# Two parts of x in one matmul of 512 columns: the up projection of a decoder layer, column tiles 6 to 21

## The chip, the cores and the metric

The kernel runs on one core of a Trainium2 chip. Its time is device time in microseconds (us) of one execution; the kernel before was run three times and once more under the hardware profiler. The engines are TensorE (PE; PEld is its weight load), VectorE (DVE), ScalarE (ACT), GpSimd (POOL) and SyncE (SP, which issues the DMAs here). Each works through its own list of instructions in order and waits on semaphores for the others.

## The reference, cut to what matters

One decoder layer on 256 rows of 1024 values in float32: a combined input projection, attention, convolution and pooling mixers, an output projection, a LayerNorm, then the gated MLP, which the change touches:

```python
x = layer_norm(DEEPNORM_ALPHA * x + mix, ln1_g, ln1_b)
up = causal_dwconv(x @ w_up, ffn_conv_w) + ffn_conv_b     # three taps along the sequence
u, g = jnp.split(up, 2, axis=-1)
ff = (u * jax.nn.silu(g)) @ w_down
return layer_norm(DEEPNORM_ALPHA * x + ff, ln2_g, ln2_b)
```

`w_up` is 1024 x 5632 (2816 columns for u, 2816 for g), `w_down` 2816 x 1024.

## The kernel before, in words

**Split products.** A float32 product is made of three matmuls in the format fp32r. Each operand a is split into a part `hi` (a copy on ScalarE that rounds, L122) and `lo` = a - hi (a subtraction on VectorE, L123); `mm3` (L149) then sums hi·hi, hi·lo and lo·hi in PSUM. Weights are split as they arrive, in units of 128 x 1024: `wsplit` (L129) issues one hi on ScalarE and one lo on VectorE. x after the first LayerNorm is split once into `xh` and `xl`.

**The MLP.** The 2816 columns of u and of g are cut into 22 column tiles of 128, j = 0 to 21. For tile j, `up_mm(j, 0)` (u) and `up_mm(j, 1)` (g) each run 8 blocks of the contraction with three matmuls of 256 columns (the sequence); the weights are the stationary operand. Both results share one PSUM bank of 512 columns. `taps(j, s)` makes the three-tap convolution: ScalarE writes y = w2·src + bias out of PSUM (L479), VectorE adds the two shifted taps (L480, L481), reading PSUM. `gate_silu` is sg on ScalarE (L485), `gate_out` is f = y0·sg on VectorE (L489), then the split of f into mh (ScalarE, L122) and ml (VectorE, L123). `down_block(k)` multiplies column tile k by its weights: matmuls of 512 columns whose stationary operand is mh or ml, summed over all tiles in four banks that stay occupied for the whole stage. Tile 0 of the up projection is computed apart (`up_first`).

**The order.** It is written out by hand. A list of blocks holds for each block its matmuls, and two lists `a` and `b` of steps for the other engines. The loop at L649 issues a block's matmuls, then the `a` steps of the block before, then weight splits as long as `ready` allows (in this stage one unit per block, six blocks ahead of its use), then the `b` steps of the block before. From tile 5 on a tile is three blocks: up u, up g, down block j - 5 (`LAG`). Down blocks 15 to 21 (`KEEP`) compute only the first half of the rows in their turn; their second half comes at the very end. The PSUM pool has eight banks, and a bank is given out again when the last reader of its old content is done.

Of the kernel before, what the change touches and what calls it, by code (L numbers as in the profile page):

```python
# [10 lines left out]
F32 = mybir.dt.float32  # L11
BF16 = mybir.dt.bfloat16
F32R = mybir.dt.float32r
AF = mybir.ActivationFunctionType
# [3 lines left out]
P = 128  # L18
D = 1024
S = 256  # L20
NT = S // P
KD = D // P
# [3 lines left out]
NJ = FF // P  # L26
# [9 lines left out]
LAG = 5  # L36
KEEP = 7
FIRST = 2
WARM = 23


PIECES = (((0, 512), (512, 512)), ((0, 512), (512, 256), (768, 256)))
# [14 lines left out]
def trunk(ctx, tc, a_qk, a_v, a_cp, a_out, a_up, a_down, x, par, tab, lnp, out):  # L57
    nc = tc.nc
    cp = ctx.enter_context(tc.tile_pool(name="cp", bufs=1))
    wp = ctx.enter_context(tc.tile_pool(name="wp", bufs=WB))  # L60
    rp = ctx.enter_context(tc.tile_pool(name="rp", bufs=RB))
    wk = ctx.enter_context(tc.tile_pool(name="wk", bufs=2))
# [3 lines left out]
    def bank():  # L66
        return ps.tile([P, 512], F32, name="bank")

    def tmp(name):
        return wk.tile([P, S], F32, name=name, tag="t", bufs=12)  # L70

# [8 lines left out]
    for n, i in units:  # L82
        at = {"qk": a_qk, "v": a_v, "cp": a_cp, "out": a_out, "u": a_up, "g": a_up, "d": a_down}[n]
        c = i if n in ("qk", "u", "g") else i // 2
        h = 0 if n in ("qk", "u") else 1 if n == "g" else i % 2
# [35 lines left out]
    def split(raw, hi, lo):  # L121
        nc.scalar.activation(hi, raw, AF.Copy)  # L122
        nc.vector.tensor_sub(lo, raw, hi.bitcast(F32))  # L123
# [25 lines left out]
    def mm3(o, lh, ll, rh, rl, start, stop, skip=False):  # L149
        for i, (l, r) in enumerate(((lh, rh), (lh, rl), (ll, rh))):  # L150
            nc.tensor.matmul(o, l, r, start=start and i == 0, stop=stop and i == 2,  # L151
                             skip_group_check=skip)

    xh = cp.tile([P, KD, S], F32R, name="xh")
    xl = cp.tile([P, KD, S], F32R, name="xl")

    zero = cp.tile([P, P], BF16, name="zero")
    nc.vector.memset(zero, 0.0)
    warm = bank()
    for i in range(WARM):  # L160
        nc.tensor.matmul(warm[:, :P], zero, zero, start=True, stop=True)
# [41 lines left out]
    mh = cp.tile([P, KD, S], F32R, name="mh")  # L203
    ml = cp.tile([P, KD, S], F32R, name="ml")
# [89 lines left out]
    def pool_sums(t, p_ps):  # L294
        p_ps = p_ps[:, :S]

        p, a, b, d = tmp("pin"), tmp("pa"), tmp("pb"), tmp("pd")
        nc.scalar.activation(p, p_ps, AF.Copy)

        def step(dst, src, w, rows):  # L300
            nc.gpsimd.tensor_add(dst[rows, w:], src[rows, w:], src[rows, :S - w])
            nc.gpsimd.tensor_copy(dst[rows, :w], src[rows, :w])

        al, up = slice(0, P), slice(DH, P)
        step(a, p, 1, al)
        if t == 0:
            step(b, a, 2, up)
        else:
            step(b, a, 2, al)
            step(a, b, 4, al)  # L310
            step(b, a, 8, up)
        iw = prm[:, C_IW + t:C_IW + t + 1]
        ed = prm[:, C_ED + 16 * t:C_ED + 16 * t + 16]
        for rows, src in ((slice(0, DH), a), (up, b)):
            nc.gpsimd.tensor_mul(d[rows, :16], src[rows, :16], ed[rows])
            nc.gpsimd.tensor_scalar(d[rows, 16:], src[rows, 16:], iw[rows], None, op0=ALU.mult)
        nc.gpsimd.tensor_sub(d, d, p)
        return d

    def pool_mm(t, d):  # L320
        y_ps = bank()
        nc.tensor.matmul(y_ps[:, :S], prm[:, C_WP + t * P:C_WP + (t + 1) * P], d,  # L322
                         start=True, stop=True)
        y = tmp("py")
        nc.scalar.activation(y, y_ps[:, :S], AF.Copy, scale=prm[:, C_PS + t:C_PS + t + 1])
        to_mix(6 + t, y)

    def conv_z(t, cc_ps, cx_ps):
        cc_ps, cx_ps = cc_ps[:, :S], cx_ps[:, :S]
        cx, z, y = tmp("cx"), tmp("cz"), tmp("cy")  # L330
        nc.scalar.activation(cx, cx_ps, AF.Copy)
        nc.vector.tensor_mul(z, cc_ps, cx)
        w = [prm[:, C_CW + 3 * t + i:C_CW + 3 * t + i + 1] for i in range(3)]
        nc.vector.tensor_scalar(y, z, w[2], None, op0=ALU.mult)
        nc.vector.scalar_tensor_tensor(y[:, 1:], z[:, :S - 1], w[1], y[:, 1:], op0=ALU.mult, op1=ALU.add)
        nc.vector.scalar_tensor_tensor(y[:, 2:], z[:, :S - 2], w[0], y[:, 2:], op0=ALU.mult, op1=ALU.add)
        return y
# [36 lines left out]
    def sum_rows(accs, rows, last, t, p, lh, ll, h, l, i):  # L374

        ts = slice(t * P, (t + 1) * P)
        if len(accs[t]) == 0:
            accs[t].extend((bank(), bank()))
        if t == 1 and p == 2 and len(accs[t]) == 2:
            accs[t].append(bank())  # L380
        whole = p is None or t == 0
        for b in range(2) if p is None else (p,):
            c, n = (b * 512, 512) if whole else PIECES[t][p]
            o = accs[t][b] if whole else accs[t][p][:, :n]
            mm3(o, lh[:, ts], ll[:, ts], h[:, c:c + n], l[:, c:c + n],
                i == 0 or (t == 1 and p == 2 and i == last), i == rows - 1, skip=True)
# [13 lines left out]
    def w_out(t, i, p):  # L400
        h, l = W["out", i]
        kt = order[i]
        sum_rows(acc, KD, FIRST, t, p, mh[:, kt], ml[:, kt], h, l, i)

# [5 lines left out]
    def w_out_last(t, p):  # L410
        for i in range(FIRST, KD):
            w_out(t, i, p)
# [39 lines left out]
    gt = {}  # L452

    def up_mm(j, s):
        h, l = W.pop(("ug"[s], j))
        if s == 0:
            u_ps[j] = bank()
        for k in range(KD):
            ws = slice(k * P, (k + 1) * P)
            mm3(u_ps[j][:, s * S:(s + 1) * S], h[:, ws], l[:, ws], xh[:, k], xl[:, k], k == 0, k == KD - 1)  # L460
# [10 lines left out]

    u_ps, ys = {}, {}

    def taps(j, s):
        c = s * NJ + j
        w = [prm[:, C_FW + 3 * c + i:C_FW + 3 * c + i + 1] for i in range(3)]
        src = u_ps[j][:, s * S:(s + 1) * S]
        y = ys[j, s] = tmp(f"y{s}")
        nc.scalar.activation(y, src, AF.Identity, scale=w[2], bias=prm[:, C_FB + c:C_FB + c + 1])  # L479
        nc.vector.scalar_tensor_tensor(y[:, 1:], src[:, :S - 1], w[1], y[:, 1:], op0=ALU.mult, op1=ALU.add)  # L480
        nc.vector.scalar_tensor_tensor(y[:, 2:], src[:, :S - 2], w[0], y[:, 2:], op0=ALU.mult, op1=ALU.add)  # L481

    def gate_silu(j):
        ys[j, 2] = tmp("sg")
        nc.scalar.activation(ys[j, 2], ys.pop((j, 1)), AF.Silu)  # L485

    def gate_out(j):
        f = tmp("f")
        nc.vector.tensor_mul(f, ys.pop((j, 0)), ys.pop((j, 2)))  # L489
        gh, gl = mh[:, j % KD], ml[:, j % KD]  # L490
        split(f, gh, gl)
        gt[j] = gh, gl

    def down(k, t, p):
        h, l = W["d", k]
# [27 lines left out]
    blocks = []  # L523

    def block(pe, need=(), a=(), b=(), now=False, hold=0, more=True):
        blocks.append((pe, list(need), list(a), list(b), now, hold, more))

    L = lambda f, *r: (lambda: f(*r))

    def seq(*fs):  # L530
        def run():
            for f in fs:
                f()
        return run
# [52 lines left out]

    for i in range(FIRST):
        block(L(w_out_first, i), [("out", i)])
    last = [("out", i) for i in range(FIRST, KD)]  # L590
    block(L(w_out_last, 0, 0), last, [L(rs, 0, 0)], hold=4)
# [15 lines left out]
    def down_unit(k):  # L607
        block(L(down_block, k), [("d", k)], hold=len(units) if k >= NJ - KEEP else 0)

    for j in range(NJ):  # L610
        gate = [L(gate_silu, j), L(gate_out, j)]
        if j == 0:
            block(seq(), (), [L(ln_rows, 0), L(taps, 0, 0), L(taps, 0, 1), L(ln1_x, 0), L(ln1_x, 1),
                              L(ln_rows, 1)], gate)
        else:
            block(L(up_mm, j, 0), [("u", j)], [L(taps, j, 0)])
            block(L(up_mm, j, 1), [("g", j)], [L(taps, j, 1)], gate)
        if j >= LAG:
            down_unit(j - LAG)
    for k in range(NJ - LAG, NJ):  # L620
        down_unit(k)
    blocks[-1][2].extend([L(rs2, 0, 0), L(rs2, 0, 1), L(ln2_out, 0)])
# [110 lines left out]
```

## Time and profile before

| | us |
|---|---|
| median of three runs | 292.94 (292.53 to 294.49) |
| the profiled execution, its own time | 291.71 |
| span from the first to the last instruction in it | 289.7 |
| TensorE busy | 280.5 |
| VectorE busy | 221.4 |
| ScalarE busy | 157.5 |
| GpSimd busy | 40.6 |

A busy time is the time in which at least one instruction of the engine is in work. Instructions on one engine overlap a little: the next starts before the record of the one ahead ends, so the distance from start to start is what an instruction takes up of its engine's time. In a timeline the bracket at the end of a row is the time for which the engine sat idle before the instruction, and what ended that.

### The profile page before, as it was taken

How to read it: one execution, taken by the hardware profiler on the slowest of the kernel's cores; microseconds unless marked ns; L12 is line 12 of the kernel's file. 1: busy time of each engine (PE TensorE's matmuls, PEld its weight loads, DVE VectorE, ACT ScalarE, POOL GpSimd, SP SyncE). 2: the span in 40 equal slices, each digit the busy share in tenths (PEclk: the TensorE clock that was granted, in tenths of full speed). 3: DMA queues.
4: the chain of work that ended last, by engine and by line, in shares of the span. 5: the costliest groups of instructions: out<-in, count | busy, mean ns of one | idle time of the engine just before them, and what ended most of it. 6: DMA issues, size and time to landing. Idle time of an engine off the chain costs nothing.

```text
span 289.7 us, 5030 instructions
## 1 busy us (share of the span) xinstructions
PE 280.5 (97%) x2032; PEld 260.9 (90%) x2032; DVE 221.4 (76%) x383; ACT 157.5 (54%) x261; POOL 40.6 (14%) x42
## 2 busy tenths in 40 slices
PE   8999999999999999999999999999999999999990
PEld 7899779999879999999999999999999999998880
DVE  2865566797948699998988888888666877768575
ACT  3844774919313384457766666666555565565100
POOL 0300005940000289700000000000000000000011
PEclk9999999999999999999999999999999999999997
DMA  7999954224980369284647484847374552100022
GB/s 279 407 362 421 410 197 148 90 83 153 382 310 1 91 221 386 74 275 143 265 147 290 148 290 146 308 149 284 133 290 147 214 223 92 53 2 0 0 76 72
DMA packets 9303, 56.21 MB, mean 194 GB/s; under 512 B 1024, under 2 KB 1280, under 8 KB 3648
## 3 DMA queue, kind: packets, MB, share of 16 engines
q1 hardware_dynamic: 7920, 50.99, 47.0%
q0 software_dynamic: 1072, 4.51, 4.5%
q10 hardware_dynamic: 288, 0.39, 0.4%
q8 instruction: 16, 0.26, 0.3%
q14 instruction: 7, 0.06, 0.1%
HBM read 54.84 MB, written 1.05 MB: 193 GB/s over the span
## 4 chain that ended last, share of the span: by engine, by line
PE 91%; issue 3%; DMA 2%; DVE 2%; POOLq 0%; POOL 0%; ACT 0%; SPq 0%; DVEq 0%
PE bank L151 84%; PE bank L468 2%; DMA raw<-a_qk 2%; PE bank L255 1%; PE bank L246 1%; PE bank L428 1%; PE bank L215 1%; DVE stat L360 1%; DVE xr L354 0%; PE bank L213 0%; DVE xr L515 0%; POOLq L729 0%; POOL mv L393 0%; PE bank L322 0%; DVE lo L123 0%
## 5 line engine op out<-in xcount | busy, mean ns | idle before, releaser
L123 DVE TENSOR_TENSOR lo<-raw,hi 128x1024 fp32r<-128x1024 f32 (+2 forms) x95 | 113.5, 1207 | 24.7 <-ACT hi L122 23.7
L151 PE MATMUL bank<-xh,hi 128*128 128x256 f32 x462 | 130.4, 282 | 0.2 <-ACT hi L122 0.2
L151 PE MATMUL bank<-xh,lo 128*128 128x256 f32 x462 | 129.0, 279 | 0.2 <-DVE lo L123 0.2
L151 PE MATMUL bank<-xl,hi 128*128 128x256 f32 x462 | 129.0, 279 | 0.0
L122 ACT ACTIVATE hi<-raw 128x1024 fp32r<-128x1024 f32 (+2 forms) x95 | 95.4, 1018 | 5.1 <-DMA raw<-a_v 4.6
L151 PEld LDWEIGHTS bank<-xh,hi 128*128 128x128 f32 x462 | 87.0, 188 | 1.8 <-issue 0.7
L151 PEld LDWEIGHTS bank<-xl,hi 128*128 128x128 f32 x462 | 87.0, 188 | 0.8
L151 PEld LDWEIGHTS bank<-xh,lo 128*128 128x128 f32 x462 | 87.0, 188 | 0.4 <-DVE lo L123 0.4
L151 PE MATMUL bank<-hi,mh 128*128 128x512 f32 (+1 forms) x133 | 49.4, 372 | 0.0
L151 PE MATMUL bank<-lo,mh 128*128 128x512 f32 (+1 forms) x133 | 49.2, 370 | 0.0
L151 PE MATMUL bank<-hi,ml 128*128 128x512 f32 (+1 forms) x133 | 49.0, 368 | 0.0
L479 ACT ACTIVATE y<-bank,prm 128x256 f32<-128x256 f32 x44 | 24.6, 560 | 25.7 <-PE bank L151 13.6
L393 POOL TENSOR_TENSOR mv<-mv,half 128x1 f32<-128x1 f32 x4 | 3.1, 776 | 186.5 <-DVE mv L392 186.5
L151 PEld LDWEIGHTS bank<-hi,ml 128*128 128x128 f32 x133 | 25.1, 188 | 4.4 <-DVE ml L123 0.2
L151 PEld LDWEIGHTS bank<-hi,mh 128*128 128x128 f32 x133 | 25.1, 189 | 4.0 <-ACT mh L122 0.4
L151 PEld LDWEIGHTS bank<-lo,mh 128*128 128x128 f32 x133 | 25.1, 189 | 3.5
L480 DVE SCALAR_TENSOR_TENSOR y<-bank,prm,y 128x255 f32<-128x255 f32 x44 | 21.1, 479 | 8.7 <-ACT y L479 8.6
L122 ACT ACTIVATE mh<-f 128x256 fp32r<-128x256 f32 x22 | 9.2, 418 | 24.3 <-DVE f L489 24.3
L481 DVE SCALAR_TENSOR_TENSOR y<-bank,prm,y 128x254 f32<-128x254 f32 x44 | 21.2, 482 | 1.6
L123 DVE TENSOR_TENSOR ml<-f,mh 128x256 fp32r<-128x256 f32 x22 | 11.0, 500 | 10.6 <-ACT mh L122 10.6
L485 ACT ACTIVATE sg<-y 128x256 f32<-128x256 f32 x22 | 9.2, 419 | 13.8 <-DVE y L481 13.8
L447 POOL TENSOR_TENSOR xr<-xr,lnp 128x1024 f32<-128x1024 f32 x2 | 13.2, 6579 | 3.4 <-DMA lnp<-lnp 3.4
(89 smaller groups left out, 198.9 us busy)
## 6 DMA issues: line engine op xcount, KB each, us to landing
raw<-a_up SPq DMA_DIRECT2D x22, 1024.0 KB, 4.9
raw<-a_down SPq DMA_DIRECT2D x11, 1024.0 KB, 5.7
raw<-a_qk SPq DMA_DIRECT2D x7, 640.0 KB, 6.7
raw<-a_cp SPq DMA_DIRECT2D x4, 1024.0 KB, 12.7
raw<-a_out SPq DMA_DIRECT2D x4, 1024.0 KB, 4.8
raw<-a_v SPq DMA_DIRECT2D x2, 1024.0 KB, 10.6
lnp<-lnp POOLq DMA_DIRECT2D x4, 512.0 KB, 4.8
bias<-tab POOLq DMA_DIRECT2D x1, 1024.0 KB, 13.5
```

The source lines that it names most:

```text
L122: nc.scalar.activation(hi, raw, AF.Copy)
L123: nc.vector.tensor_sub(lo, raw, hi.bitcast(F32))
L151: nc.tensor.matmul(o, l, r, start=start and i == 0, stop=stop and i == 2, skip_group_check=skip)
L215: nc.tensor.matmul(s_ps[h][:, P:P + S], qT[r, j, 1], kT[r, j], start=True, stop=True)
L246: nc.tensor.transpose(t_ps[:, i * P:(i + 1) * P], pr[:, i * P:(i + 1) * P], ident)
L393: nc.gpsimd.tensor_tensor(mv[:, 2:], mv[:, 2:], half, op=ALU.pow)
L447: nc.gpsimd.tensor_mul(xr[:, t], xr[:, t], gb[0][:, 0])
L468: nc.tensor.matmul(u_ps[0][:, c:c + P], part(("ug"[s], 0))[:, k * P:(k + 1) * P], xf[:, k, t * P:(t + 1) * P], start=t == 0 and n == 0, st ...
L479: nc.scalar.activation(y, src, AF.Identity, scale=w[2], bias=prm[:, C_FB + c:C_FB + c + 1])
L480: nc.vector.scalar_tensor_tensor(y[:, 1:], src[:, :S - 1], w[1], y[:, 1:], op0=ALU.mult, op1=ALU.add)
L481: nc.vector.scalar_tensor_tensor(y[:, 2:], src[:, :S - 2], w[0], y[:, 2:], op0=ALU.mult, op1=ALU.add)
L485: nc.scalar.activation(ys[j, 2], ys.pop((j, 1)), AF.Silu)
```

## The change

For column tiles 6 to 21 (`TWIN`) the parts xh and xl of x lie side by side in one tile `xp`, and an up step runs two matmuls per contraction block instead of three: hi against both parts, 512 columns, and lo against xh, 256 columns. The two halves of the result lie in one bank, u and g in a bank each. `twin_sum` copies the half hi·xl to SBUF on ScalarE (e) and adds it to the other on VectorE (us); the taps read us from SBUF. The pool of temporaries has 14 buffers instead of 12. In these tiles the steps are also attached otherwise: the sum is an `a` step of the up block, the taps are `b` steps; silu is an `a` step and f a `b` step of the down block behind; the split of f is an `a` step of the next tile's first block.

```diff
+TWIN = 6
+TMP = 14
...
-    xh = cp.tile([P, KD, S], F32R, name="xh")
-    xl = cp.tile([P, KD, S], F32R, name="xl")
+    xp = cp.tile([P, KD, 2, S], F32R, name="xp")
+    xh, xl = xp[:, :, 0], xp[:, :, 1]
...
     def up_mm(j, s):
         h, l = W.pop(("ug"[s], j))
+        if j >= TWIN:
+            o = u_ps[j, s] = bank()
+            for k in range(KD):
+                ws = slice(k * P, (k + 1) * P)
+                nc.tensor.matmul(o, h[:, ws], xp[:, k], start=k == 0, stop=False, skip_group_check=True)
+                nc.tensor.matmul(o[:, :S], l[:, ws], xh[:, k], start=False, stop=k == KD - 1,
+                                 skip_group_check=True)
+            return
...
+    def twin_sum(j, s):
+        o = u_ps.pop((j, s))
+        e, u = tmp("e"), tmp("us")
+        nc.scalar.activation(e, o[:, S:], AF.Copy)
+        nc.vector.tensor_add(u, o[:, :S], e)
+        us[j, s] = u
...
-        src = u_ps[j][:, s * S:(s + 1) * S]
+        src = us.pop((j, s)) if j >= TWIN else u_ps[j][:, s * S:(s + 1) * S]
...
-        else:
+        elif j < TWIN:
             block(L(up_mm, j, 0), [("u", j)], [L(taps, j, 0)])
             block(L(up_mm, j, 1), [("g", j)], [L(taps, j, 1)], gate)
+        else:
+            block(L(up_mm, j, 0), [("u", j)],
+                  [L(gate_split, j - 1)] * (j > TWIN) + [L(twin_sum, j, 0)], [L(taps, j, 0)])
+            block(L(up_mm, j, 1), [("g", j)], [L(twin_sum, j, 1)], [L(taps, j, 1)])
         if j >= LAG:
             down_unit(j - LAG)
+            if j >= TWIN:
+                blocks[-1][2].append(L(gate_silu, j))
+                blocks[-1][3].append(L(gate_mul, j))
+    blocks[-1][3].append(L(gate_split, NJ - 1))
```

`gate_mul` is the product f, `gate_split` its split into mh and ml; together they are the old `gate_out`.

ScalarE, one column tile in the middle of the stage, before; y is the first tap of u and then of g, sg the silu, mh the high part of f, and each hi a weight split:

```order
L122 ACTIVATE mh<-f 128x256
L122 ACTIVATE hi<-raw 128x1024
L479 ACTIVATE y_2357<-bank,prm 128x256
L122 ACTIVATE hi<-raw 128x1024
L479 ACTIVATE y_2379<-bank,prm 128x256
L122 ACTIVATE hi<-raw 128x1024
L485 ACTIVATE sg<-y_2379 128x256
```

And of the change, where e is the copy of the second half out of PSUM and us the sum:

```order
L124 ACTIVATE mh<-f 128x256
L490 ACTIVATE e<-bank 128x256
L124 ACTIVATE hi<-raw 128x1024
L501 ACTIVATE y_2216<-us,prm 128x256
L490 ACTIVATE e<-bank 128x256
L124 ACTIVATE hi<-raw 128x1024
L501 ACTIVATE y_2244<-us,prm 128x256
L507 ACTIVATE sg<-y_2244 128x256
L124 ACTIVATE hi<-raw 128x1024
```

Two copies e are new, each y has moved behind a hi, and sg has moved from behind the third hi to ahead of it.

VectorE, one column tile from the split of f on, before; each lo is a weight split and the two rows of y behind it are the second and third tap:

```order
L123 TENSOR_TENSOR ml<-f,mh 128x256
L123 TENSOR_TENSOR lo<-raw,hi 128x1024
L480 SCALAR_TENSOR_TENSOR y_2177<-bank,prm,y_2177 128x255
L481 SCALAR_TENSOR_TENSOR y_2177<-bank,prm,y_2177 128x254
L123 TENSOR_TENSOR lo<-raw,hi 128x1024
L480 SCALAR_TENSOR_TENSOR y_2199<-bank,prm,y_2199 128x255
L481 SCALAR_TENSOR_TENSOR y_2199<-bank,prm,y_2199 128x254
L123 TENSOR_TENSOR lo<-raw,hi 128x1024
L489 TENSOR_TENSOR f<-y_2177,sg 128x256
```

And of the change:

```order
L125 TENSOR_TENSOR ml<-f,mh 128x256
L491 TENSOR_TENSOR us<-bank,e 128x256
L125 TENSOR_TENSOR lo<-raw,hi 128x1024
L502 SCALAR_TENSOR_TENSOR y_2216<-us,prm,y_2216 128x255
L503 SCALAR_TENSOR_TENSOR y_2216<-us,prm,y_2216 128x254
L491 TENSOR_TENSOR us<-bank,e 128x256
L125 TENSOR_TENSOR lo<-raw,hi 128x1024
L502 SCALAR_TENSOR_TENSOR y_2244<-us,prm,y_2244 128x255
L503 SCALAR_TENSOR_TENSOR y_2244<-us,prm,y_2244 128x254
L125 TENSOR_TENSOR lo<-raw,hi 128x1024
L511 TENSOR_TENSOR f<-y_2216,sg 128x256
```

VectorE keeps the order of its old instructions; a us has come ahead of the first lo and ahead of the second.

## Rows read from the trace of the kernel before

**Rows 1.** The page, busy us, share of the span, instructions.

```profile
PE 280.5 (97%) x2032; PEld 260.9 (90%) x2032; DVE 221.4 (76%) x383; ACT 157.5 (54%) x261; POOL 40.6 (14%) x42
```

**Rows 2.** Timeline of TensorE: start us, us, engine, line, op, out<-in.

```profile
134.36 0.28 PE L151 MATMUL bank<-xh,hi 128*128 128x256 f32 x1
...
142.71 0.28 PE L151 MATMUL bank<-xh,hi 128*128 128x256 f32 x1
...
258.20 0.28 PE L151 MATMUL bank<-xh,hi 128*128 128x256 f32 x1
...
263.81 0.39 PE L151 MATMUL bank<-hi,mh 128*128 128x512 f32 x1
...
270.63 0.39 PE L151 MATMUL bank<-hi,mh 128*128 128x512 f32 x1
...
281.66 0.28 PE L151 MATMUL bank<-hi,ml 128*128 128x256 f32 x1
```

**Rows 3.** Timeline of VectorE over one column tile.

```profile
174.92 0.42 DVE L489 TENSOR_TENSOR f<-y,sg 128x256 f32<-128x256 f32 x1
...
176.78 1.23 DVE L123 TENSOR_TENSOR lo<-raw,hi 128x1024 fp32r<-128x1024 f32 x1 [0.53 <-ACT hi L122]
177.92 0.48 DVE L480 SCALAR_TENSOR_TENSOR y<-bank,prm,y 128x255 f32<-128x255 f32 x1
178.43 0.48 DVE L481 SCALAR_TENSOR_TENSOR y<-bank,prm,y 128x254 f32<-128x254 f32 x1
178.83 1.22 DVE L123 TENSOR_TENSOR lo<-raw,hi 128x1024 fp32r<-128x1024 f32 x1
179.96 0.48 DVE L480 SCALAR_TENSOR_TENSOR y<-bank,prm,y 128x255 f32<-128x255 f32 x1
180.48 0.48 DVE L481 SCALAR_TENSOR_TENSOR y<-bank,prm,y 128x254 f32<-128x254 f32 x1
180.88 1.22 DVE L123 TENSOR_TENSOR lo<-raw,hi 128x1024 fp32r<-128x1024 f32 x1
182.01 0.42 DVE L489 TENSOR_TENSOR f<-y,sg 128x256 f32<-128x256 f32 x1
```

**Rows 4.** Timeline of ScalarE over the same tile.

```profile
175.38 0.42 ACT L122 ACTIVATE mh<-f 128x256 fp32r<-128x256 f32 x1 [0.99 <-DVE f L489]
175.70 1.04 ACT L122 ACTIVATE hi<-raw 128x1024 fp32r<-128x1024 f32 x1
176.65 0.55 ACT L479 ACTIVATE y<-bank,prm 128x256 f32<-128x256 f32 x1
...
181.05 0.42 ACT L485 ACTIVATE sg<-y 128x256 f32<-128x256 f32 x1 [0.59 <-DVE y L481]
```

**Rows 5.** Operations of the convolution mixer: ns min/median/max, first and last start us, forms.

```profile
L331 ACT ACTIVATE cx<-bank x2: 367/368/368, 57.0 to 68.8; 128x256 f32<-128x256 f32 x2
L332 DVE TENSOR_TENSOR cz<-bank,cx x2: 409/412/415, 59.5 to 71.7; 128x256 f32<-128x256 f32 x2
...
L336 DVE SCALAR_TENSOR_TENSOR cy<-cz,prm,cy x2: 483/484/484, 61.5 to 73.1; 128x254 f32<-128x254 f32 x2
```

**Rows 6.** Timeline of VectorE around f of tile 5 and of tile 21.

```profile
146.58 0.42 DVE L489 TENSOR_TENSOR f<-y,sg 128x256 f32<-128x256 f32 x1
...
148.44 1.23 DVE L123 TENSOR_TENSOR lo<-raw,hi 128x1024 fp32r<-128x1024 f32 x1 [0.53 <-ACT hi L122]
...
268.32 0.43 DVE L489 TENSOR_TENSOR f<-y,sg 128x256 f32<-128x256 f32 x1 [0.55 <-ACT sg L485]
```

**Rows 7.** Stretches behind the last matmul: TensorE busy, granted clock, DMA share, GB/s.

```profile
284.00:285.00 1.00, 0.00 (x0) 1.00 0.00 0
285.00:286.00 1.00, 0.00 (x0) 0.95 0.00 0
286.00:289.00 3.00, 0.00 (x0) 0.50 0.50 175
```

**Rows 8.** Timeline of TensorE, start of the span.

```profile
0.99 2.63 PE L161 MATMUL bank<-zero 128*128 128x128 bf16 x23 [0.99 <-DVE half L163]
...
6.09 0.28 PE L151 MATMUL bank<-xh,hi 128*128 128x256 f32 x1
```

More of the change, by code (lines that the diff above doesn't have):

```diff
@@ L69, in tmp @@
     def tmp(name):
-        return wk.tile([P, S], F32, name=name, tag="t", bufs=12)
+        return wk.tile([P, S], F32, name=name, tag="t", bufs=TMP)
     units = [("qk", k) for k in range(KD)]
@@ L472, in trunk @@
     u_ps, ys = {}, {}
+    def twin_sum(j, s):
[4 more added lines that the diff above has]
+        us[j, s] = u
+    us = {}
     def taps(j, s):
@@ L485, in gate_silu, with gate_mul, gate_split @@
         nc.scalar.activation(ys[j, 2], ys.pop((j, 1)), AF.Silu)
-    def gate_out(j):
[L488 to L492, printed above, removed]
+    def gate_mul(j):
+        ys[j, 3] = tmp("f")
+        nc.vector.tensor_mul(ys[j, 3], ys.pop((j, 0)), ys.pop((j, 2)))
+    def gate_split(j):
+        gt[j] = mh[:, j % KD], ml[:, j % KD]
+        split(ys.pop((j, 3)), *gt[j])
+    def gate_out(j):
+        gate_mul(j)
+        gate_split(j)
     def down(k, t, p):
```

## The prediction

> **What bounds the kernel now.** I read the busy times first, then TensorE's timeline, then the timelines of VectorE and ScalarE over one column tile. TensorE is busy 97% of the span [rows 1], and in the up projection it has no idle time: the tile that begins at 134.36 us gives way to the next at 142.71, a pitch of 8.35 us [rows 2]. The 48 matmuls of 256 columns from 258.20 to 263.81 are 0.117 us apart, the 30 of 512 columns from 263.81 to 270.63 are 0.227 apart [rows 2]: columns are paid for, with 0.007 us saved when two 256s become one 512. So today TensorE sets the end.
>
> The second thing to see is how near the pair ScalarE/VectorE is behind it. One tile goes from gate product f at 174.92 to the next f at 182.01, 7.09 us [rows 3]. VectorE there waits for no matmul, since y (ScalarE's first tap) of this tile follows its hi split without a pause [rows 4]. So 7.09 us is the pair's own pace, and it is a loop that can be added up from start to start: f to mh 0.46, mh to hi 0.32, hi to lo 1.08, lo to first tap 1.14, tap to tap 0.51, tap to lo 0.40, lo to tap 1.13, tap to tap 0.52, tap to lo 0.40, lo to f 1.13 [rows 3, 4]. Sum 7.09. The pair runs faster than TensorE only because the third lo need not wait: ScalarE made its hi while VectorE did the second taps.
>
> The pair is also late when the changed tiles begin. f of tile 5 stands at 146.58 and the lo after it at 148.44 [rows 6], yet TensorE began tile 6 at 134.36 [rows 2]. It is some 11 us behind and now wins back 8.35 - 7.09 = 1.26 us per tile. At the end f of tile 21 starts at 268.32 [rows 6] and the last down block, which needs it, at 270.63 [rows 2]. After mh (0.46 + 0.46) only 1.4 us are spare.
>
> **The change, part by part.**
>
> TensorE, tiles 6 to 21: 3 x 0.117 = 0.351 becomes 0.227 + 0.117 = 0.344 us for each of 16 x 2 x 8 = 256 groups. That is 0.0065 x 256 = 1.7 us saved, all of it on today's path.
>
> Two copies e and two additions us per tile. A copy of 128x256 out of PSUM takes 0.37 us, an addition with one operand in PSUM 0.41 [rows 5]. Following instructions start 0.10 before the end on ScalarE (mh: 0.42 long, next after 0.32; hi: 1.04 and 0.95) and 0.08 on VectorE (second tap: 0.48 and 0.40) [rows 3, 4]. So I charge 0.27 for an e and 0.33 for a us in their engine's queue. The Trainium skill, page "ScalarE: Activation LUTs", section "What ACT_TABLE_LOAD costs", gives 186 ns + 0.833 ns per element with an overlap of about 93 ns, hence 0.31 us for e (an estimate); by it the result below would be 0.6 us later, and no run here times this copy in this place.
>
> Taps that read SBUF in place of PSUM: the same operation from SBUF took 0.484 us [rows 5] against 0.48 now [rows 3], so nothing. y, whether quicker or not, is ready before the lo ahead of the taps is done.
>
> The order is what costs. ScalarE's order per tile is now e, hi, y, e, hi, y, sg, hi, mh: silu (sg) stands ahead of the third hi, and sg must wait for the second taps of the same tile. VectorE's third lo then waits for sg and hi in turn. The loop becomes: f to mh 0.46, mh to e 0.32, e to hi 0.27, hi to lo 1.08, lo to tap 1.14, 0.51, tap to us 0.40, us to lo 0.33, lo to tap 1.13, 0.52, tap to sg 0.57 (180.48 to 181.05 [rows 3, 4]), sg to hi 0.32 (as mh to hi), hi to lo 1.08, lo to f 1.13. Sum **9.26 us per tile**: +0.27 for e, +0.33 for us, +1.57 where 0.57 + 0.32 + 1.08 replace 0.40. The other e and us lie beside splits. The loop is closed (the next e is behind mh), so no run-ahead shortens it; and it is longer than TensorE's new pitch of 8.35 - 0.10 = 8.25.
>
> The stretch of tiles 6 to 21: the lo at 148.44 stays; us follows at 149.57, the next lo at 149.90, f of tile 6 after 7.13 more at 157.03. Fourteen loops of 9.26 bring f of tile 20 to 286.67. Tile 21 has no third split: 4.18 to its second us, then us to y 0.46, y 0.55 and 0.04 to the tap (hi, 1.04 long, lets lo go after 1.08), 0.52, 0.57, sg to f 0.45: f at 293.4, mh at 293.9, and the last down block may start at **294.4** instead of 270.63. That is +23.7 us; what follows it is unchanged. The 1.7 us of TensorE are lost, since it no longer sets the end.
>
> What TensorE does meanwhile: each up step now takes a bank of its own, four of the eight stay with the down sums, so a step waits for the us of the same half two tiles before. The first us (149.57 + 0.41) still precedes tile 8 (150.96), but 1.0 us is lost per tile, so from tile 9 or 10 on there is a pause of about 1 us per tile. These pauses are not on the path. At the end there are two long ones: down block 20 waits for mh of tile 20 until 287.6, though block 19 ends about 281 (up step 21 starts after us of tile 19, 272.8, plus 2.75 and four blocks of 1.36), and block 21 until 294.4.
>
> TensorE's clock after these two pauses: the granted clock was full until 285, four microseconds after the last matmul at 281.66 [rows 2, 7], and then 0.50, which is 1.2 GHz. The first of the two pauses, 6.6 us, is longer than that. At the start of the trace 23 matmuls of 128 columns took 2.63 us, 0.114 each, and the pitch of 0.12 for 256 columns is reached by 6.09 [rows 8], five microseconds after the first. Half of the work in such a stretch is lost: 0 if the clock holds, at most 2.5 us. I take 2. The page "TensorE: Matmul & The Clock Gate" of the Trainium skill, section "Part 1: The HAM clock gate", says that an idle engine goes back to half rate and has the full rate again only after it has been busy for a while. By that rule the 2 us are owed, and the fall to 0.50 behind the last matmul agrees; how the clock returns after a pause no trace here shows. If it did not fall at all, the time would be 2 us less.
>
> **Sum.** 291.71 us is this profiled execution's own time; + 23.7 + 2 = 317.4. It stands 1.23 below the median of the runs, 292.94, so for the median **318.6**.
>
> **Bounds.** If the two charged operations together cost 0.2 less per tile and the clock holds: -0.2 x 15 - 2, about 313.5. If neither overlaps its successor (0.37 and 0.41): +0.18 x 15 = 2.7, and a little more clock, about 323. Far ends: VectorE's own work without a wait is 3 x 1.13 + 2 x 0.92 + 2 x 0.33 + 2 x 0.33 = 6.55 us per tile, in which case TensorE's saving shows, 291.3; and with whole durations one after the other (no overlaps at all) the loop is about 10.0, + 11, 330.
>
> **Rivals.**
>
> *The loop keeps up (not slower), 7%.* Mechanism: the third hi does not cost VectorE a wait, because sg finds its taps done. The loop is then 9.26 - 1.57 = 7.69, and the last down block can start at 164.7 + 14 x 7.69 = 272.4: 294.7 for the median; with e and us hidden as well, TensorE stays the bound at 292.94 - 1.7 = 291.3. It decides where the loop is below 7.8 us (there the end is 1% later than now; equal at 7.57). For it: 7.09 now, and VectorE still waits 0.53 before one lo of the tile [rows 3]. Against it: sg reads what the second taps write, and ScalarE stood idle 0.59 before sg for just that [rows 4].
>
> *The loop is shorter than summed, 8%:* some operations in the new order overlap more, 8.2 to 8.7 us; 14 x 0.56 to 1.06 less, so 304 to 311. For it: all joints are taken from one tile of the old order. Against it: the same joints give 7.09 exactly.
>
> *The clock falls in the pauses of each tile, 2%.* A tile's matmuls at 1.2 GHz need 16.5 us, longer than the loop; twelve tiles would add 87 us, about 400. Against it: the clock outlasted four idle microseconds [rows 7]; the pauses are 1.
>
> **Numbers.** The forecast has 83%; with its bounds, 313 to 324, and the shorter loop I give 309 to 325. Within 1% (what a measurement of this kernel can tell from no change, 3 us) only the first rival lies, nearly whole: same 7%, faster 1%, slower 92%.
>
> **What would show it.** In the changed profile: f to f about 9.26 us from tile 6 on; VectorE idle about 1.5 us before the third lo, released by ScalarE's hi, and ScalarE idle before sg; TensorE pausing about 1 us before an up step from tile 9 or 10 on, released by us, and twice for several microseconds before down blocks 20 and 21; 0.344 us for a 512 and a 256. If f to f is below 7.8, or the third hi starts before the second taps end, the prediction is wrong.

## The result, and the profile after

The changed kernel takes 318.92 us (median of 5 runs, 318.62 to 320.59) against 292.94: 1.0898 times the time before, 95% interval 1.0852 to 1.0944. The forecast was 318.6 in a range of 309 to 325. The profiled execution took 318.72 us with a span of 316.7, 27.0 more than before.

The page first: busy us, the granted clock in 40 slices, and the shares of the chain that ended last; the last row is that chain in the kernel before.

```profile
PE 290.7 (92%) x1776; PEld 251.5 (79%) x1776; DVE 232.4 (73%) x415; ACT 166.2 (52%) x293; POOL 40.9 (13%) x42
...
PEclk9999999999999999999999999999999999996598
...
DVE 54%; ACT 23%; issue 9%; DMA 6%; PE 5%; POOL 0%; SPq 0%; POOLq 0%; DVEq 0%; ACTq 0%
...
PE 91%; issue 3%; DMA 2%; DVE 2%; POOLq 0%; POOL 0%; ACT 0%; SPq 0%; DVEq 0%
```

TensorE is no longer busy throughout [rows 1 had 97%], yet no other engine is busier in share than it was: VectorE fell from 76 to 73%. The busy shares would not name the bound. The chain points to it: before, it ran 91% on TensorE, and now 54% on VectorE and 23% on ScalarE, so it passes to and fro between two engines of which neither is full.

VectorE over one changed tile, answering to rows 3 (the bracket is the idle time before a row and what ended it):

```profile
222.22 0.42 DVE L511 TENSOR_TENSOR f<-y,sg 128x256 f32<-128x256 f32 x1
...
226.40 0.42 DVE L491 TENSOR_TENSOR us<-bank,e 128x256 f32<-128x256 f32 x1
226.74 1.21 DVE L125 TENSOR_TENSOR lo<-raw,hi 128x1024 fp32r<-128x1024 f32 x1
...
228.38 0.48 DVE L503 SCALAR_TENSOR_TENSOR y<-us,prm,y 128x254 f32<-128x254 f32 x1
230.36 1.23 DVE L125 TENSOR_TENSOR lo<-raw,hi 128x1024 fp32r<-128x1024 f32 x1 [1.50 <-ACT hi L124]
231.50 0.42 DVE L511 TENSOR_TENSOR f<-y,sg 128x256 f32<-128x256 f32 x1
```

From f to f it is 9.28 us. Before the third lo VectorE waits 1.50 us for ScalarE's hi; in rows 3 that lo followed the tap at once. ScalarE in the same tile, answering to rows 4, shows why:

```profile
228.96 0.42 ACT L507 ACTIVATE sg<-y 128x256 f32<-128x256 f32 x1 [1.50 <-DVE y L503]
229.28 1.04 ACT L124 ACTIVATE hi<-raw 128x1024 fp32r<-128x1024 f32 x1
231.95 0.42 ACT L124 ACTIVATE mh<-f 128x256 fp32r<-128x256 f32 x1 [1.63 <-DVE f L511]
232.28 0.37 ACT L490 ACTIVATE e<-bank 128x256 f32<-128x256 f32 x1
232.54 1.05 ACT L124 ACTIVATE hi<-raw 128x1024 fp32r<-128x1024 f32 x1
```

ScalarE stands idle for 1.50 us in front of sg, with the hi for VectorE queued behind it; when VectorE has done its taps, both sg and hi have to pass before VectorE can go on. Each waits for the other in turn.

f of tiles 6, 7, 20 and 21, on VectorE's timeline [rows 6]:

```profile
157.01 0.42 DVE L511 TENSOR_TENSOR f<-y,sg 128x256 f32<-128x256 f32 x1
...
166.57 0.42 DVE L511 TENSOR_TENSOR f<-y,sg 128x256 f32<-128x256 f32 x1
...
287.14 0.42 DVE L511 TENSOR_TENSOR f<-y,sg 128x256 f32<-128x256 f32 x1
293.94 0.43 DVE L511 TENSOR_TENSOR f<-y,sg 128x256 f32<-128x256 f32 x1 [0.54 <-ACT sg L507]
```

TensorE's timeline, an up step in the stage, down block 18 waiting for its own weight split, the starts of the last two down blocks, the return of the pitch, and the last matmul [rows 2]:

```profile
223.94 0.50 PE L464 MATMUL bank<-xp,hi 128*128 128x512 f32 x1 [0.57 <-DVE us L491]
...
280.01 0.50 PE L153 MATMUL bank<-hi,mh 128*128 128x512 f32 x1 [0.58 <-ACT hi L124]
...
288.06 0.79 PE L153 MATMUL bank<-hi,mh 128*128 128x512 f32 x1 [3.00 <-ACT mh L124]
...
294.87 0.80 PE L153 MATMUL bank<-hi,mh 128*128 128x512 f32 x1 [3.89 <-ACT mh L124]
295.46 0.63 PE L153 MATMUL bank<-lo,mh 128*128 128x512 f32 x1
295.89 0.63 PE L153 MATMUL bank<-hi,ml 128*128 128x512 f32 x1
...
300.16 0.52 PE L153 MATMUL bank<-hi,mh 128*128 128x512 f32 x1
...
308.66 0.28 PE L153 MATMUL bank<-hi,ml 128*128 128x256 f32 x1
```

The last down block starts 24.24 us later than before (294.87 against 270.63). From it to the last matmul it is 13.79 us against 11.03 (281.66 - 270.63 [rows 2]), since the matmuls are 0.43 us apart until 300.16. 24.24 + 2.76 is the whole 27.0. The granted clock says the same; the columns are the stretch, its length, busy us and count of PE, PEld, DVE, ACT and POOL, the clock, and the DMA's share and GB/s:

```profile
284.00:286.00 2.00, 1.06 (x5) 0.55 (x3) 0.49 (x2) 1.36 (x2) 0.00 (x0) 1.00 0.01 4
286.00:288.00 2.00, 0.00 (x0) 0.00 (x0) 1.56 (x2) 0.41 (x2) 0.00 (x0) 0.69 0.00 0
...
298.00:300.00 2.00, 2.00 (x6) 1.60 (x5) 1.90 (x7) 0.00 (x0) 0.00 (x0) 0.50 0.00 0
300.00:302.00 2.00, 2.00 (x9) 1.60 (x9) 2.00 (x4) 0.00 (x0) 1.00 (x1) 0.90 0.00 0
```

### The profile page after: what moved, and what is told of

Its sections match the earlier page's. It is cut to its first block, busy times and chain, and to the rows that moved or that the text cites. A ratio compares the mean times of both kernels' runs of the same rounds, so it can differ in the third digit from the quotient of the medians.

```text
span 316.7 us, 4587 instructions
## 1 busy us (share of the span) xinstructions
PE 290.7 (92%) x1776; PEld 251.5 (79%) x1776; DVE 232.4 (73%) x415; ACT 166.2 (52%) x293; POOL 40.9 (13%) x42
## 4 chain that ended last, share of the span: by engine, by line
DVE 54%; ACT 23%; issue 9%; DMA 6%; PE 5%; POOL 0%; SPq 0%; POOLq 0%; DVEq 0%; ACTq 0%
DVE lo L125 29%; ACT hi L124 13%; DVE y L502 5%; DVE y L503 5%; PE bank L153 5%; DMA raw<-a_v 4%; ACT mh L124 3%; DVE f L511 3%; ACT sg L507 2%; DMA raw<-a_qk 2%; DVE us L491 2%; ACT pr L231 2%; ACT e L490 1%; DVE pr L239 1%; DVE xp L125 1%
## 5 line engine op out<-in xcount | busy, mean ns | idle before, releaser
L464 PE MATMUL bank<-xp,hi 128*128 128x512 f32 x256 | 92.8, 401 | 7.9 <-DVE us L491 7.8
L153 PE MATMUL bank<-xp,hi 128*128 128x256 f32 x412 | 74.5, 284 | 0.0
L465 PE MATMUL bank<-xp,lo 128*128 128x256 f32 x256 | 72.0, 281 | 0.0
L464 PEld LDWEIGHTS bank<-xp,hi 128*128 128x128 f32 x256 | 48.0, 188 | 25.1 <-DVE us L491 15.3
L153 PEld LDWEIGHTS bank<-xp,hi 128*128 128x128 f32 x412 | 63.7, 190 | 1.0 <-issue 0.7
L153 PE MATMUL bank<-hi,mh 128*128 128x512 f32 (+1 forms) x133 | 51.4, 386 | 7.6 <-ACT mh L124 6.9
L153 PE MATMUL bank<-xp,lo 128*128 128x256 f32 x206 | 57.9, 281 | 0.1
L153 PE MATMUL bank<-lo,mh 128*128 128x512 f32 (+1 forms) x133 | 50.9, 383 | 1.6 <-DVE lo L125 1.5
L153 PE MATMUL bank<-hi,ml 128*128 128x512 f32 (+1 forms) x133 | 50.5, 380 | 0.0
L465 PEld LDWEIGHTS bank<-xp,lo 128*128 128x128 f32 x256 | 48.3, 189 | 0.2
L153 PEld LDWEIGHTS bank<-xp,lo 128*128 128x128 f32 x206 | 39.0, 189 | 0.3 <-DVE lo L125 0.3
L501 ACT ACTIVATE y<-us,prm 128x256 f32<-128x256 f32 x32 | 19.1, 597 | 14.4 <-DVE us L491 14.4
L503 DVE SCALAR_TENSOR_TENSOR y<-us,prm,y 128x254 f32<-128x254 f32 x32 | 15.4, 483 | 1.1
```

The costliest lines, as they stand in the source:

```text
L464: nc.tensor.matmul(o, h[:, ws], xp[:, k], start=k == 0, stop=False, skip_group_check=True)
L465: nc.tensor.matmul(o[:, :S], l[:, ws], xh[:, k], start=False, stop=k == KD - 1, skip_group_check=True)
```

## The experiments

The theory: silu ahead of the third hi closes a loop of 9.27 us per tile between ScalarE and VectorE. The rivals: the banks (each half holds one now), the added e and us, or the wider matmuls. Ratios are against runs of the kernel before on the same chip, with the 95% interval; an execution may come to this stage some 3 us later than another (in the trace of the first experiment f of tile 5 stands at 149.83, after TensorE had waited 2.35 us for a split near 10 us and then worked at a granted clock of 0.50 from 12 to 14 us), so times within a trace are compared from f of tile 5 on (146.58 before, 146.54 in the changed kernel).

**Silu moved back, all else as changed.**

```diff
-                blocks[-1][2].append(L(gate_silu, j))
-                blocks[-1][3].append(L(gate_mul, j))
+                blocks[-1][3].extend([L(gate_silu, j), L(gate_mul, j)])
```

> Only silu moves: behind the third weight split, ahead of f, as in the kernel before; the 512-column matmuls, the copies e, the sums us and a bank for each half stay. Theory (silu ahead of the third hi closes a loop between ScalarE and VectorE): the loop loses 0.57 + 0.32 + 1.08 and gets 0.40 back, 9.27 - 1.57 = 7.70 us from f to f as long as the pair is behind TensorE, no wait of 1.5 us before the third lo; f of tile 20 near 263, of tile 21 near 270, the last down block near 271, within half a microsecond of where it stood before the change: 292 to 295 us. Rival (the new banks hold TensorE: an up step waits for us of two tiles before, or the extra e and us themselves are the load): nothing of that is changed here, so the time stays above 310.

Measured: 293.23 us, 1.0009 (0.9975 to 1.0042): the whole loss is gone. VectorE, the third lo and f:

```profile
197.19 0.42 DVE L511 TENSOR_TENSOR f<-y,sg 128x256 f32<-128x256 f32 x1
...
203.34 0.48 DVE L503 SCALAR_TENSOR_TENSOR y<-us,prm,y 128x254 f32<-128x254 f32 x1
203.74 1.22 DVE L125 TENSOR_TENSOR lo<-raw,hi 128x1024 fp32r<-128x1024 f32 x1
204.88 0.42 DVE L511 TENSOR_TENSOR f<-y,sg 128x256 f32<-128x256 f32 x1
```

The lo follows the tap after 0.40 without a wait, and f of the tile before stood at 197.19, 7.69 us earlier. The chain that ended last still runs 46% on VectorE and 12% on ScalarE here, so where the chain lies does not by itself mean time lost; the distance from f to f does. The rivals that keep the banks, e, us and the wide matmuls as the cause fall.

**The order alone, without wide matmuls, e and us.**

```diff
-        if j >= TWIN:
+        if False:
             o = u_ps[j, s] = bank()
...
     def twin_sum(j, s):
+        return
...
-        src = us.pop((j, s)) if j >= TWIN else u_ps[j][:, s * S:(s + 1) * S]
+        src = u_ps[j][:, s * S:(s + 1) * S]
```

> The steps stand in the changed order (silu ahead of the third split, taps behind their split, f's split in the next tile), but the up projection is the old one: three matmuls of 256, u and g in one bank, no e, no us. Theory: the loop is 7.09 + 1.57 = 8.66 us per tile, above TensorE's 8.35; f of tile 20 near 278, the last down block near 285 in place of 270.6, two pauses of TensorE behind the last up step and a low clock there: 306 to 311 us. Rival (banks and sums are the cost): no banks and no sums are left, so 293.

Measured: 308.74 us, 1.0534 (1.0485 to 1.0584). VectorE from one f to the next:

```profile
243.54 0.42 DVE L512 TENSOR_TENSOR f<-y,sg 128x256 f32<-128x256 f32 x1
...
251.07 1.23 DVE L125 TENSOR_TENSOR lo<-raw,hi 128x1024 fp32r<-128x1024 f32 x1 [1.50 <-ACT hi L124]
252.21 0.42 DVE L512 TENSOR_TENSOR f<-y,sg 128x256 f32<-128x256 f32 x1
```

8.67 us, with the same wait of 1.50. So the order makes 1.58 of the loop (8.67 - 7.09) and e with us the remaining 0.61 (9.28 - 8.67); with silu moved back, where of the loop's additions only e and us are left, it is 0.60 (7.69 - 7.09). These are the two terms of the sum, measured apart. In ScalarE's list each y stands behind a hi already before the change; of the old steps silu alone changes its place there. So the 1.58 is the price of silu ahead of the third hi.

**The wide matmuls alone,** with the old order; the product of hi with the low part of x is left out of the result.

```diff
-        src = us.pop((j, s)) if j >= TWIN else u_ps[j][:, s * S:(s + 1) * S]
+        src = u_ps[j, s][:, :S] if j >= TWIN else u_ps[j][:, s * S:(s + 1) * S]
```

(and the blocks, silu and f as in the kernel before)

> The matmuls of the change alone: hi against both parts in 512 columns, lo against 256, u and g in a bank each, with the old order of all steps. The taps read only the first half of the bank, so the product hi with the low part of x is left out of the sum (no e, no us). Theory: TensorE saves 256 x 0.0065 = 1.7 us and nothing else moves: 291.3 us, matmuls 0.227 and 0.117 apart. Rival: a bank for each half makes TensorE wait for the taps of two tiles before, which run late in tiles 6 to 9; then no gain or some loss, 293 to 296.

Measured: 292.4 us, 0.998 (0.9947 to 1.0014), no difference that can be told. The trace is sharper. TensorE within an up step, and from one down block to the next:

```profile
201.90 0.40 PE L464 MATMUL bank<-xp,hi 128*128 128x512 f32 x1
202.14 0.28 PE L465 MATMUL bank<-xp,lo 128*128 128x256 f32 x1
...
203.65 0.39 PE L464 MATMUL bank<-xp,hi 128*128 128x512 f32 x1
...
224.07 0.39 PE L153 MATMUL bank<-hi,mh 128*128 128x512 f32 x1
...
232.37 0.39 PE L153 MATMUL bank<-hi,mh 128*128 128x512 f32 x1
```

Five groups of 512 + 256 take 1.75 us (201.90 to 203.65), 0.350 each, where three 256s took 0.351 and I had summed 0.344. The tile takes 8.30 in place of 8.35: at most 0.8 us over 16 tiles, half of the expected gain. A 512 in this place costs 0.233, not 0.227.

**Dummy matmuls in TensorE's two last pauses,** 40 ahead of each of down blocks 20 and 21, writing a bank that nobody reads.

```diff
     def down_block(k):
+        if k >= NJ - 2:
+            for _ in range(40):
+                nc.tensor.matmul(fill[0][:, :P], zero, zero, start=True, stop=True)
```

> The changed kernel, with 40 matmuls of a zero tile (128 columns) ahead of down block 20 and 40 ahead of down block 21, where TensorE waits for mh. They write a bank that nobody reads. Theory (half of the work behind these pauses runs at 1.2 GHz): the clock stays full or nearly so, the matmuls from 294.9 on run 0.227 apart at once, about 2.4 us less: 316.5 us. Rival (the clock there costs nothing, the rest of the tail hides it): 318.9.

The last down block's first matmul and the last matmul of all:

```profile
295.89 0.80 PE L153 MATMUL bank<-hi,mh 128*128 128x512 f32 x1 [2.93 <-ACT mh L124]
...
308.40 0.28 PE L153 MATMUL bank<-hi,ml 128*128 128x256 f32 x1
```

Measured: 318.59 us, 1.0852 (1.0807 to 1.0897): no clear gain. The clock stayed full in the first pause, but 2.9 us of the second were left idle and it fell there; the last down block began 1.0 us later than in the changed kernel because the execution as a whole ran late (f of tile 5 at 147.49). From it to the last matmul the trace has 12.51 us in place of 13.79, so 1.3 us were won back and the late start hides them in the time. The number of dummies was set too low.

**The same with 64 ahead of the last block.**

```diff
-            for _ in range(40):
+            for _ in range(40 if k == NJ - 2 else 64):
```

> As e4, with 40 matmuls of the zero tile ahead of down block 20 and 64 ahead of down block 21, so that the second pause too is filled to within a microsecond. In e4 the clock stayed full through the first pause but fell in the 2.9 us that were left idle of the second. Theory: full clock from the last down block on, its 30 matmuls and those behind it 0.227 and 0.12 apart; from that block to the last matmul 11.0 us as in the kernel before, in place of 13.8: 2.7 us less than the changed kernel, 316. Rival: the end does not follow, 318.9.

Measured: 317.27 us, 1.0828 (1.0785 to 1.0871). TensorE and its clock:

```profile
295.61 0.50 PE L153 MATMUL bank<-hi,mh 128*128 128x512 f32 x1 [1.55 <-ACT mh L124]
...
306.77 0.28 PE L153 MATMUL bank<-hi,ml 128*128 128x256 f32 x1
```

```profile
296.00:298.00 2.00, 2.00 (x10) 1.62 (x9) 1.29 (x4) 0.00 (x0) 0.00 (x0) 1.00 0.00 0
```

From the last block to the last matmul it is 11.16 us in place of 13.79, so in the trace the clock's share is 2.6 us, and the rest of the end follows. Between the two medians the time fell by only 1.65, where 2.7 were expected; in the trace the last block began 0.74 later, as f of tile 5 had (147.25 against 146.54). The two intervals overlap, so the trace carries this, not the ratio.

**The new form only from tile 14 on.**

```diff
-TWIN = 6
+TWIN = 14
```

> The changed kernel with TWIN = 14: only tiles 14 to 21 have the new form. Theory (a loop of 9.27 us per tile that begins where the first changed tile begins): by tile 13 the pair has caught up with TensorE, so the loop starts without the 11 us of delay; f of tile 14 near 213.8, of tile 20 near 269.4, of tile 21 near 276.2, the last down block near 277 in place of 270.6: 6.4 us later, 299 us, or up to 302 if the clock falls before it. Rival (a cost for each changed tile, whatever the state at their start): half of the tiles, half of the 26 us: 306.

Measured: 301.44 us, 1.0276 (1.0236 to 1.0315). VectorE at the start of the new form and at its end:

```profile
204.86 0.42 DVE L511 TENSOR_TENSOR f<-y,sg 128x256 f32<-128x256 f32 x1
215.33 0.42 DVE L511 TENSOR_TENSOR f<-y,sg 128x256 f32<-128x256 f32 x1
...
271.01 0.42 DVE L511 TENSOR_TENSOR f<-y,sg 128x256 f32<-128x256 f32 x1
```

TensorE at the last down block:

```profile
278.75 0.80 PE L153 MATMUL bank<-hi,mh 128*128 128x512 f32 x1 [5.15 <-ACT mh L124]
```

From f of tile 13 to f of tile 20 it is 66.15 us (I had 66.1 from 203.32 to 269.4). The last down block began at 278.75 after 5.15 us without a matmul, 6.6 us later against f of tile 13 than before, and the rest, to 291.38, took 12.63 in place of 11.03. Half of the tiles cost a third of the loss, 8.3 of 26 us, since they start without the 11 us of delay: the cost is not so much per tile but what the loop loses against TensorE, less what is spare at the start. The rival's 306 is out.

**The split of f moved as well,** behind the next tile's first weight split, with silu behind the third.

```diff
-                  [L(gate_split, j - 1)] * (j > TWIN) + [L(twin_sum, j, 0)], [L(taps, j, 0)])
+                  [L(twin_sum, j, 0)], [L(gate_split, j - 1)] * (j > TWIN) + [L(taps, j, 0)])
```

> Silu behind the third split as in e1, and the split of f (mh, ml) behind the next tile's first weight split instead of ahead of e: ScalarE's order is e, hi, mh, y, e, hi, y, hi, sg. Theory: now no wait of VectorE closes the loop; it takes its own work, 6.6 us per tile, so the 11 us of delay are won back by tile 13 and TensorE alone sets the end. With the 8.30 us per tile of e3 the time is 0.8 us under the kernel before: 292.1, which 5 rounds may just not tell from 292.9. Rival (the twin sums cost TensorE something in any order): 293.5 or more.

Measured: 292.5 us, 0.9979 (0.9954 to 1.0003). VectorE early in the stage and late in it:

```profile
165.41 0.42 DVE L511 TENSOR_TENSOR f<-y,sg 128x256 f32<-128x256 f32 x1
...
172.04 0.42 DVE L511 TENSOR_TENSOR f<-y,sg 128x256 f32<-128x256 f32 x1
...
239.60 0.42 DVE L511 TENSOR_TENSOR f<-y,sg 128x256 f32<-128x256 f32 x1
240.99 0.42 DVE L491 TENSOR_TENSOR us<-bank,e 128x256 f32<-128x256 f32 x1 [0.97 <-ACT e L490]
...
247.90 0.42 DVE L511 TENSOR_TENSOR f<-y,sg 128x256 f32<-128x256 f32 x1
```

6.63 us per tile with no wait left early; later f is 8.30 apart and VectorE waits for e, which waits for TensorE. The new form fits under TensorE in this order. Whether it beats the kernel before is not shown: the interval reaches 1.0003, and the next run, which changes nothing on a path, gave the same ratio.

**Only the layout of x and 14 temporaries,** in the old form.

```diff
-TWIN = 6
+TWIN = 99
```

(without the `gate_split` behind the loop)

> The kernel before with only the layout of x (both parts in one tile) and 14 temporaries instead of 12; no tile has the new form. Theory: neither is on a path: 292.9, pitch of TensorE 8.35 us per tile. Rival (reading x from the joint tile changes the pace of TensorE): another pitch.

Measured: 292.83 us, 0.9979 (0.9953 to 1.0005); f from tile 14 to 20 at 213.12 to 263.20, 8.35 us apart. Neither costs or gives anything, and a ratio of 0.998 here is no gain.

**Runs of one width,** on top of the version with silu and the split of f moved: the eight wide matmuls of an up step one behind the other, then the eight of 256.

```diff
             for k in range(KD):
                 ws = slice(k * P, (k + 1) * P)
                 nc.tensor.matmul(o, h[:, ws], xp[:, k], start=k == 0, stop=False, skip_group_check=True)
+            for k in range(KD):
+                ws = slice(k * P, (k + 1) * P)
                 nc.tensor.matmul(o[:, :S], l[:, ws], xh[:, k], start=False, stop=k == KD - 1,
```

> As e6, with the eight matmuls of 512 columns of an up step one behind the other and then the eight of 256, in place of the alternation. In the alternation a group of both takes 0.350 us, where the rows of the kernel before add up to 0.227 + 0.117 = 0.344. Theory: the 0.006 are lost where the widths change, so in runs of one width the group takes 0.344, the tile 8.25 us in place of 8.30: 0.8 us less than e6, 291.5 to 292. Rival: a matmul of 512 that reads x takes 0.233 wherever it stands: tile 8.30, time as e6.

Measured: 293.63 us, 1.0035 (1.0005 to 1.0066), a little slower. TensorE over one tile:

```profile
219.37 2.03 PE L464 MATMUL bank<-xp,hi 128*128 128x512 f32 x8
221.24 1.11 PE L467 MATMUL bank<-xp,lo 128*128 128x256 f32 x8
...
224.99 0.40 PE L153 MATMUL bank<-hi,mh 128*128 128x512 f32 x1
```

Eight 512s take 1.87 us, 0.234 each. My theory that the change of width costs the 0.006 falls. But the tile took 8.40 (216.59 to 224.99), and the down block behind it too was slower (12 matmuls in 2.78 us, 216.59 to 219.37), which the rival does not explain either.

## Why the prediction was right

*The bound changes hands.* It did, and by the loop as summed: 9.26 us per tile from joints of the old order, 9.28 measured; 8.66 and 8.67 without e and us; 7.70 and 7.69 with silu moved back. The joints between engines, taken from start to start in one tile, carry over to another order.

*The stretch.* f of tile 6 at 157.03 was measured at 157.01, of tile 20 at 286.67 against 287.14, the last down block at 294.4 against 294.87. Of this half microsecond 0.30 comes from tile 7, whose loop took 9.56 (157.01 to 166.57), since sg started late there; why stays open. The rest is 0.01 to 0.02 in each of the thirteen other loops. The two charged operations cost what was charged: from start to start e took 0.26 us (232.28 to 232.54) and us 0.34 (226.40 to 226.74) for 0.27 and 0.33, so the estimate of 0.31 for e was too long.

*The clock.* I took 2 and called 2.5 the most; it was 2.8 by the trace, so the term was too small and its bound wrong, and the filled pauses gave 2.6 of it back. The sum was 25.7 for the profiled execution, 27.0 was measured: 0.5 from the stretch, 0.8 from the clock. The fall to half rate in an idle engine that the Trainium skill, page "TensorE: Matmul & The Clock Gate", section "Part 1: The HAM clock gate", states agrees in kind with this trace: 0.69 from 286 to 288 without a matmul, 0.50 from 298 to 300 still, and rising behind it.

*TensorE's pauses.* The wait for us came once per tile, with 0.57 us idle in the record, and from tile 10 on. The first long pause was misjudged: I had TensorE waiting idle from 281 to 287.6, but it stood only 3.00 us before block 20, since down blocks 17 to 19 had already waited for their own hi and lo, which the same loop made late. My argument for the fall was that a pause of 6.6 us is longer than the four idle microseconds that the clock had outlasted [rows 7]. The pauses were 3.00 and 3.89 us, both shorter, and by that argument the clock would have held. That it fell nevertheless, and that the term of 2 came out near, was luck.

*TensorE's saving of 1.7 us* was mis-sized: 0.350 us per group was measured for 0.344, 8.30 per tile for 8.25, so 0.8 at most. The forecast did not depend on it, as another engine sets the end.

*The rivals.* That the loop keeps up did not happen in this order; in the version that moves silu back it does, at 293.2 where the prediction had 294.7 for that mechanism. Its sum took the 1.57 off fourteen loops and left it in tile 6, where the run shows it gone too: f of tile 6 came 8.89 us behind f of tile 5 (149.83 to 158.72), against 10.47 in the changed kernel. The shorter loop and the clock falling in each tile's pause did not occur: the clock was full through the stage.

## What to carry to other kernels

Where two engines hand work to each other, write down their instruction orders for one period and add up, from start to start, the path that returns to itself; if it is longer than the period of the bounding engine, that path is the new bound, though neither engine is busy more than three quarters. An instruction that must wait for the other engine belongs behind those that the other engine waits for, not ahead. And a delay that is hidden today (here 11 us at tile 6) counts in full once the pair no longer wins it back.

## What the runs showed of the hardware that was not expected

A matmul of 512 columns took 0.227 us in the down blocks and 0.233 to 0.234 in the up steps, alternating or not, so two 256s in one instruction saved next to nothing (2 x 0.117 is 0.234); with runs of one width the down blocks slowed to 0.232 as well. No run tells why. The clock fell within a pause of 3.0 us (0.69 from 286 to 288), ahead of which TensorE had paused three times between 279 and 284 (idle 0.58, 0.76 and 0.72), while in the kernel before it outlasted more than three idle microseconds behind dense work [rows 2, 7]; no run tells what makes the difference. The 0.43 pitch lasted 5.3 us from the last down block's start.
